# The mixers' output projection in seven products, and split input weights kept for the second half

## The chip, the core and the metric

The kernel runs on one core of one Trainium2 chip. A core has TensorE (matmuls and transposes), VectorE, ScalarE, GpSimd (POOL) and SyncE (SP, which issues most of the transfers here); each works through its own queue of instructions in order, and waits on semaphores for the others. Sixteen DMA engines move data between the device's memory (DRAM, in the program's names) and the on-chip memory. The metric is the device time of one execution in microseconds (us), median of three runs for the kernel before.

## The reference: what is computed

One decoder layer on 1024 tokens of width 1024, in float32. Four blocks follow each other, each with a residual sum and a layer norm:

```
h = LN1(a*h + 1/2 SwiGLU_1(h))                 w_gate, w_up: 1024 x 2816, w_down: 2816 x 1024
h = LN2(a*h + concat(o_a, o_b) @ w_out)        proj = h @ w_in  (1024 x 3072); w_out: 1024 x 1024
h = LN3(a*h + CrossAttention(h, LN(mem)))      4 heads of 256, 256 memory tokens; output weights w_o
h = LN4(a*h + 1/2 SwiGLU_2(h))
```

The second block is that of the "mixers". Of `proj`, 512 columns each are the query, the forget gate, the value and the output gate of a gated linear recurrence (HGRN2) with four heads of 128, and 2 x 512 are the two inputs of a spatial gate. `o_a` is the recurrence's output, normalised and multiplied by silu of the output gate; it needs every earlier token. `o_b` is the spatial gate's output, in blocks of 128 tokens. Both together, 1024 columns, go through `w_out`.

## The kernel before

Operands are held as pairs. A float32 value is split into a rounded part `hi` (type fp32r, a copy on ScalarE, line 114) and the rest `lo` (a subtraction on VectorE, line 115); a product of two such pairs is three matmuls, hi*hi, hi*lo and lo*hi, added up in PSUM (`mm3`, lines 137 to 139). The tokens' activations lie transposed in `xh[half]` and `xl[half]`, two halves of 512 tokens. Weights come through three rings of on-chip tiles: `raw` (three tiles), `whi` (six) and `wlo` (five). A tile is loaded only when the ring's oldest user is done with it.

Some large products are made with seven products of blocks in place of eight (Strassen's scheme in Winograd's form). In the two FFNs that is so for the gate, up and down projections, and in the cross attention for the output projection by `w_o` (class `Square`). For `Square` the weights' seven combined blocks are made ahead, during the first FFN, by `later`, `square_operands` and `prepare`: POOL and SP build four sums of weight blocks in DRAM (`steps`: copies on SP, accumulating transfers on POOL), and item by item a raw block is loaded (line 286), copied to `hi` and to `-hi` on ScalarE (lines 293 and 294) and written to `sq_ops` in DRAM (297); an accumulating transfer of POOL adds the raw block onto `-hi`, which gives `lo` (302). Each item, eighteen with those for the second FFN, takes 16 units of the planned time. `Square` then loads finished pairs with `fetch_parts`.

The output projection of the mixers is the plain eight. `down_group` runs over groups of token tiles, (0, 1), (2, 3, 4) and (5, 6, 7); for each of eight row blocks of `w_out` it loads and splits the block, and multiplies. So `w_out` is loaded and split three times, 24 blocks. `residual_norm` then loads the residual, adds, normalises and transposes.

The mixers go by halves, `m0` and `m1`. A "unit" is 24 matmuls of 512 columns: 24 units a half for the six groups of 512 columns. The weights of each unit or group of four are loaded and split (`load_split`) in each half, so that `w_in` is split twice. The recurrence of a head (`recurrence`) is a flow: a generator that emits its instructions a step at a time, as the units' planned time (`tick`) goes on. The order of the last part is `m1.body()`, the projection of tiles 0 and 1, `m1.tail()` (the output gate's units), `drain()` (all flows to their end), and the projection of the other tiles. Then the cross attention works on half `F = 0` first and on half `G = 1` after it.

The order of instructions on every engine is laid out when the program is built, by a planner that starts from the program's order and its own estimates of time. Instructions marked `pinned` keep their order among themselves. On the chip each queue is worked off in that order, whatever is late.

Of the kernel before, what the change touches and what calls it, by code (L numbers as in the profile page):

```python
# [15 lines left out]
P = 128  # L16
# [18 lines left out]
def hybrid_layer_kernel(ctx: ExitStack, tc: tile.TileContext, a, out):  # L35
# [184 lines left out]
    def residual_norm(tt, lag, acc, res_src, gb, bb, dst, name, keep=None):  # L220

        r = gt(f"r_{name}")
        nc.sync.dma_start(r, res_src[tt * P:(tt + 1) * P, :])
        for dh in range(2):
            sl = slice(dh * 512, (dh + 1) * 512)
            nc.vector.scalar_tensor_tensor(r[:, sl], r[:, sl], ALPHA, acc[dh], op0=ALU.mult, op1=ALU.add)
        layer_norm(r, gb, bb, name)
        nc.sync.dma_start(dst[tt * P:(tt + 1) * P, :], r)
        yield lag
        yield from to_xT_steps(r, tt, list(range(KT)), name, keep, 2.6)  # L230

    def down_group(w, nk, grp, operand, res_src, gb, bb, dst, name, keep=None):

        acc = {tt: [ps_mm(f"acc_{name}_{tt}_{dh}") for dh in range(2)] for tt in grp}
        for k in range(nk):
            wh, wl = load_split(w[k * P:(k + 1) * P, :], f"wd_{name}_{grp[0]}_{k}")
            ops = operand(grp, k)
            for tt in grp:
                oh, ol = ops[tt]
                for dh in range(2):  # L240
                    sl = slice(dh * 512, (dh + 1) * 512)
                    mm3(acc[tt][dh], oh, ol, wh[:, sl], wl[:, sl], k == 0, k == nk - 1)
            yield 1.3 * len(grp)
        for i, tt in enumerate(grp):
            spawn(residual_norm(tt, 6 + 4.5 * i, acc[tt], res_src, gb, bb, dst, f"{name}_{tt}", keep))

    def run(flow):
        for us in flow:
            tick(us)

    def xT_operand(grp, k):
        return {tt: (xh[tt // 4][:, k, (tt % 4) * P:(tt % 4 + 1) * P],
                     xl[tt // 4][:, k, (tt % 4) * P:(tt % 4 + 1) * P]) for tt in grp}

# [6 lines left out]
    def square_operands(w, ops, name):  # L261
# [11 lines left out]
        for p, first, b in ((7, 3, (0, 1)), (6, 7, (0, 0)), (4, 6, (1, 0)), (5, 1, (0, 1))):  # L273
# [4 lines left out]
                 f"{name}_{p}{n}") for p in (1, 2, 3, 7, 6, 4, 5) for n in range(2)]  # L278
# [234 lines left out]
    def strassen(wc, rhs, name):  # L513
# [26 lines left out]
        nc.vector.tensor_tensor(b0, b0, product(4), op=ALU.subtract)  # L540
        yield

    def ffn(wg, wu, wd, g, b, res_src, dst, make_xT, xf, name, start=None, h0=0):


        wc = {}
# [919 lines left out]
```

## Time and profile before

| | |
|---|---|
| runs | 2033.49, 2034.85, 2037.83 us; median 2034.85 |
| profiled execution | 2037.76 us, its span 2036.0 us |
| mean granted TensorE clock | 0.995 |
| busy share of the span | TensorE 99%, VectorE 73%, ScalarE 45%, POOL 7% |
| moved by DMA | 361.41 MB, 178 GB/s on average |
| matmuls | 9598 |

The span runs from the first to the last instruction of one execution. A matmul's busy time overlaps that of the next, so the time of many is read from a stretch, not from the sum of their durations. The wait that is put to an engine names what came last before it could go on. A waiting engine costs time only where the chain that ends last runs through it.

### The profile page before, as it was taken

How to read it: one execution, taken by the hardware profiler on the slowest of the kernel's cores; microseconds unless marked ns; L12 is line 12 of the kernel's file. 1: busy time of each engine (PE TensorE's matmuls, PEld its weight loads, DVE VectorE, ACT ScalarE, POOL GpSimd, SP SyncE). 2: the span in 40 equal slices, each digit the busy share in tenths (PEclk: the TensorE clock that was granted, in tenths of full speed). 3: DMA queues.
4: the chain of work that ended last, by engine and by line, in shares of the span. 5: the costliest groups of instructions: out<-in, count | busy, mean ns of one | idle time of the engine just before them, and what ended most of it. 6: DMA issues, size and time to landing. Idle time of an engine off the chain costs nothing.

```text
span 2036.0 us, 25494 instructions
## 1 busy us (share of the span) xinstructions
PE 2009.1 (99%) x9598; PEld 1681.2 (83%) x9598; DVE 1490.1 (73%) x2238; ACT 917.3 (45%) x1279; POOL 140.7 (7%) x187
## 2 busy tenths in 40 slices
PE   8999999999999999999999999999999999999998
PEld 7888878888887888888888888888888888888786
DVE  5977677777667967857796854678776776776688
ACT  6634344434443557647654343434333233244332
POOL 0001010120001110100110100010000000000021
PEclk9999999999999999999999999999999999999999
DMA  8369998867877642223146434652332332378874
GB/s 270 125 196 257 262 271 247 239 150 242 283 276 264 226 140 73 63 62 94 52 156 224 158 114 145 218 206 104 117 106 88 121 103 88 126 246 286 281 250 169
DMA packets 267674, 361.41 MB, mean 178 GB/s; under 512 B 16224, under 2 KB 160224, under 8 KB 267488
## 3 DMA queue, kind: packets, MB, share of 16 engines
q1 hardware_dynamic: 257216, 346.16, 50.5%
q0 software_dynamic: 10336, 13.63, 4.6%
q8 instruction: 75, 1.23, 0.2%
q14 instruction: 47, 0.39, 0.1%
HBM read 267.99 MB, written 109.58 MB: 185 GB/s over the span
## 4 chain that ended last, share of the span: by engine, by line
PE 82%; DMA 5%; DVE 4%; issue 1%; ACT 1%; POOL 0%; SPq 0%; POOLq 0%; DVEq 0%; ACTq 0%
PE dp_f L137 6%; PE dp_f L138 6%; PE dp_f L139 6%; PE st_uf L139 5%; PE st_uf L138 5%; PE st_uf L137 5%; PE st_gf L139 5%; PE st_gf L138 5%; PE st_gf L137 5%; PE psl L1168 2%; DMA wg_f_r<-in_ffn_w_gate_dram 1%; PE paq L137 1%; PE paq L139 1%; PE paq L138 1%; PE acc_mx L137 1%; PE acc_mx L138 1%
## 5 line engine op out<-in xcount | busy, mean ns | idle before, releaser
L138 PE MATMUL dp_f<-wd_f_l,ah_f 128*128 128x512 f32 x552 | 213.3, 390 | 0.0
L137 PE MATMUL dp_f<-wd_f_h,ah_f 128*128 128x512 f32 x552 | 208.5, 390 | 0.6 <-ACT ah_f L114 0.6
L139 PE MATMUL dp_f<-wd_f_h,al_f 128*128 128x512 f32 x552 | 206.1, 390 | 0.6 <-DVE al_f L115 0.5
L139 PEld LDWEIGHTS dp_f<-wd_f_h,al_f 128*128 128x128 f32 x552 | 103.6, 188 | 22.7 <-DVE al_f L115 1.4
L137 PEld LDWEIGHTS dp_f<-wd_f_h,ah_f 128*128 128x128 f32 x552 | 103.6, 188 | 22.3 <-ACT ah_f L114 1.0
L138 PEld LDWEIGHTS dp_f<-wd_f_l,ah_f 128*128 128x128 f32 x552 | 103.6, 188 | 21.4
L114 ACT ACTIVATE wd_f_h<-wd_f_r 128x1024 fp32r<-128x1024 f32 x72 | 73.2, 1022 | 99.5 <-DVE wd_f_r L651 29.1
L115 DVE TENSOR_TENSOR al_f<-ar_f,ah_f 128x1024 fp32r<-128x1024 f32 x72 | 84.5, 1174 | 27.6 <-ACT ah_f L114 27.0
L114 ACT ACTIVATE ah_f<-ar_f 128x1024 fp32r<-128x1024 f32 x72 | 73.4, 1020 | 67.0 <-DMA ar_f<-lops 64.9
L115 DVE TENSOR_TENSOR wd_f_l<-wd_f_r,wd_f_h 128x1024 fp32r<-128x1024 f32 x72 | 84.3, 1175 | 11.6 <-ACT wd_f_h L114 11.5
L137 PE MATMUL st_uf<-xh,wu_f_h 128*128 128x512 f32 x168 | 66.2, 394 | 2.7 <-ACT wu_f_h L114 2.7
L138 PE MATMUL st_uf<-xl,wu_f_h 128*128 128x512 f32 x168 | 66.0, 393 | 0.0
L139 PE MATMUL st_uf<-xh,wu_f_l 128*128 128x512 f32 x168 | 65.4, 393 | 0.1
L137 PE MATMUL st_gf<-xh,wg_f_h 128*128 128x512 f32 x168 | 65.4, 389 | 0.0
L138 PE MATMUL st_gf<-xl,wg_f_h 128*128 128x512 f32 x168 | 65.4, 389 | 0.0
L139 PE MATMUL st_gf<-xh,wg_f_l 128*128 128x512 f32 x168 | 64.7, 389 | 0.0
L775 POOL TENSOR_SCALAR nm_f<-nm_f 128x1 f32<-128x1 f32 x8 | 9.7, 1215 | 775.3 <-ACT xl L774 775.3
L531 DVE TENSOR_TENSOR top_uf<-bot_uf,st_uf 128x512 f32<-128x512 f32 x21 | 14.4, 686 | 65.5 <-PE st_uf L139 50.9
L115 DVE TENSOR_TENSOR wu_f_l<-wu_f_r,wu_f_h 128x1024 fp32r<-128x1024 f32 x42 | 51.2, 1219 | 9.7 <-ACT wu_f_h L114 9.7
L114 ACT ACTIVATE wu_f_h<-wu_f_r 128x1024 fp32r<-128x1024 f32 x42 | 44.1, 1051 | 24.2 <-issue 17.7
L529 ACT ACTIVATE bot_gf<-st_gf 128x512 f32<-128x512 f32 x21 | 12.5, 594 | 93.1 <-PE st_gf L139 93.1
L114 ACT ACTIVATE wg_f_h<-wg_f_r 128x1024 fp32r<-128x1024 f32 x42 | 44.1, 1051 | 22.2 <-PE st_gf L138 15.6
(497 smaller groups left out, 6001.0 us busy)
## 6 DMA issues: line engine op xcount, KB each, us to landing
ar_f<-lops SPq DMA_DIRECT2D x66, 512.0 KB, 5.1
wd_f_r<-in_ffn_w_down_dram SPq DMA_DIRECT2D x56, 512.0 KB, 4.9
wg_f_r<-in_ffn_w_gate_dram SPq DMA_DIRECT2D x42, 512.0 KB, 3.9
wu_f_r<-in_ffn_w_up_dram SPq DMA_DIRECT2D x42, 512.0 KB, 4.5
wd_mx_r<-in_w_out_dram SPq DMA_DIRECT2D x24, 512.0 KB, 3.9
lops<-bot_gf SPq DMA_DIRECT2D x21, 512.0 KB, 4.3
lops<-top_uf SPq DMA_DIRECT2D x21, 512.0 KB, 4.1
lops<-bot_uf SPq DMA_DIRECT2D x21, 512.0 KB, 4.7
```

Of the source, the lines that this page charges most:

```text
L114: order(nc.scalar.activation(hi, src, AF.Copy))
L115: order(nc.vector.tensor_tensor(lo, src, hi.bitcast(F32), op=ALU.subtract))
L137: nc.tensor.matmul(ps, lh, rh, start=first, stop=False, skip_group_check=more)
L138: nc.tensor.matmul(ps, lh, rl, start=False, stop=False, skip_group_check=more)
L139: nc.tensor.matmul(ps, ll, rh, start=False, stop=last, skip_group_check=more)
L529: nc.scalar.activation(b0, product(1), AF.Copy)
L531: nc.vector.tensor_tensor(t0, b0, product(2), op=ALU.add)
L775: nc.gpsimd.tensor_scalar(nmean, nmean, -1.0 / D, None, op0=ALU.mult)
L1168: nc.tensor.matmul(psl[:m, (i * NC2 + c) * 64:(i * NC2 + c + 1) * 64] .rearrange("p (n b) -> p n b", b=B), e[:, :m], blk(e, B)[:, :, 1, :] ...
```

## The change

First, the output projection becomes a `Square` named `msq`. Its left operands are the gated outputs (`o_a`, rows 0 to 511 of the contraction, and `o_b`, the rest) of the first half (kept in DRAM as `oa_dram` for use again) and of the second half. Products 2 and 1 need the first half alone and are emitted after `m1.tail()`; 7, 4, 6, 5 and 3 come after `drain()`. The second half is finished first (after product 5), the first half last (after product 3), and the cross attention takes `F = 1`, `G = 0`, so that the second half comes first there. `w_out` is no longer loaded in the mixers; its seven combined blocks, 14 items, are made in the first FFN with those of `w_o`, but with `hi` on ScalarE and `lo` on VectorE and without POOL's accumulation. With 32 items in place of 18, an item takes 12 units of planned time and the first begins 20 units earlier.

Second, the first half writes the split pairs of `w_in` to DRAM (`in_parts`), and the second half loads the pairs, with no split of its own. In the second half's body the last recurrence is started ahead of the four `vs` units, not after two of them.

```diff
-        todo = [(... ops[p - 1, n], f"{name}_{p}{n}") for p in (1, 2, 3, 7, 6, 4, 5) for n in range(2)]
+        todo = [(... ops[p - 1, n], f"{name}_{p}{n}", name == "mx") for p in (1, 2, 3, 7, 6, 4, 5) for n in range(2)]
...
         yield 16
-        for k, (src, dst, name) in enumerate(todo):
+        for k, (src, dst, name, by_vector) in enumerate(todo):
+            if by_vector:
+                hi, lo = (wpool.tile(list(src.shape), F32R, tag=f"w{i}", bufs=n, name=f"p{i}_{name}")
+                          for i, n in (("hi", 6), ("lo", 5)))
+                split(raw, hi, lo, pinned)
+                yield 3
+                for d, t in zip(dst, (hi, lo)):
+                    pinned(nc.sync.dma_start(d, t.bitcast(F32)))
+                raw = load(k + 1)
+                if steps:
+                    steps.pop(0)()
+                yield 9
+                continue
...
-            yield 4
+            yield 3
...
-            yield 12
+            yield 9
...
     def later():
-        yield 40
+        yield 20
...
-        for n, w in (("xa", a["xa_w_o"][0]),):
+        for n, w in (("mx", a["w_out"][0]), ("xa", a["xa_w_o"][0]),):
             t, s = square_operands(w, sq_ops[n], n)
-            todo += t
+            todo.append(t)
             steps += s
+        todo = todo[0][:6] + todo[1][:6] + todo[0][6:] + todo[1][6:]
...
+    def in_parts(half, view, name, key):
+        if half:
+            return fetch_parts(in_ops[key], name)
+        parts = load_split(view, name)
+        in_ops[key] = [dram.tile([P] + list(view.shape[1:]), F32, name=f"in_{name}_{i}") for i in range(2)]
+        for d, t in zip(in_ops[key], parts):
+            nc.sync.dma_start(d, t.bitcast(F32))
+        return parts
...
-            to_xT(o, self.half * NC2 + i, [0, 1, 2, 3], f"oa{self.half}{i}")
...
+            if self.half:
+                for n in range(2):
+                    if i == 0:
+                        msq.s[n] = gt(f"s3_mx{n}", (P, 2, HALF))
+                        msq.a1[0][n] = mixed_again(0, n)
+                    nc.vector.tensor_tensor(msq.s[n][:, :, cs], msq.a1[0][n][:, :, cs],
+                                            ptv[:, 2 * n:2 * n + 2, :], op=ALU.subtract)
+                    if last:
+                        msq.put(msq.s[n], 1, 0, n)
+                        msq.put(self.u[n], 1, 4, n)
+                        nc.vector.tensor_tensor(msq.s[n], msq.s[n], self.u[n], op=ALU.add)
+                return
+            split(ptv, xh[0][:, 0:4, cs], xl[0][:, 0:4, cs])
...
-    run(mix_group((0, 1)))
     play(m1.tail())
+    msq.fetch(2, 1)
+    x = msq.bank("sx2")
+    for n in range(2):
+        msq.step(2, x, 0, 4, n, True)
+    msq.p2 = msq.copies(x, "p2")
+    x = msq.bank("sx")
+    for n in range(2):
+        msq.step(1, x, 0, 0, n, True)
+    msq.fetch(7)
...
+    for t in range(4):
+        msq.residual(msq.top, 0, t)
+        msq.onto(msq.top[t][:, 0], msq.p2[t], ALU.add, ALPHA)
+        msq.onto(msq.top[t][:, 0], x[t])
+        msq.onto(msq.top[t][:, 1], x[t], ALU.subtract, ALPHA)
     drain()
-    run(mix_group((2, 3, 4)))
-    run(mix_group((5, 6, 7)))
-    F, G = 0, 1
+    for n in range(2):
+        msq.step(7, x, 1, 0, n)
+    msq.fetch(4)
+    msq.finish(x, msq.p2)
+    F, G = 1, 0
```

More of the change, by code (lines that the diff above doesn't have):

```diff
@@ L218, in layer_norm @@
         ln_apply(y, stt, gb, bb, name)
[L220 to L253, printed above, removed]
     pinned = tc.keep_in_program_order
@@ L541, in strassen, with ffn @@
         yield
-    def ffn(wg, wu, wd, g, b, res_src, dst, make_xT, xf, name, start=None, h0=0):
+    def ffn(wg, wu, wd, g, b, res_src, dst, make_xT, xf, name, start=None):
         wc = {}
@@ L1027, in feat_unit @@
     def feat_unit(half, c, name, evac):
-        evac(feat_group(load_split(wcol(w_in, c), f"{name}{half}"), half, f"ps_{name}{half}"))
+        evac(feat_group(in_parts(half, wcol(w_in, c), f"{name}{half}", c), half, f"ps_{name}{half}"))
     class Mixers:
```

53 lines of the change are left out of this document (36 added, 17 removed).

## The prediction

> **What bounds the kernel now.** I read the page first, then TensorE's waits, then the stretches of time, and last the rows of single stalls.
>
> ```profile
> span 2036.0 us, 25494 instructions
> PE 2009.1 (99%) x9598; PEld 1681.2 (83%) x9598; DVE 1490.1 (73%) x2238; ACT 917.3 (45%) x1279; POOL 140.7 (7%) x187
> q1 hardware_dynamic: 257216, 346.16, 50.5%
> q0 software_dynamic: 10336, 13.63, 4.6%
> ...
> PE dp_f L137 <- DVE db_f L798: 4.8, 2, 3.0
> PE st_uf L137 <- ACT wu_f_h L114: 2.7, 1, 2.7
> ...
> PE st_uf L137 <- DVE bot_gf L536: 0.9, 1, 0.9
> ...
> PE psl L1168 <- DVE r_mx L226: 0.4, 1, 0.4
> ```
>
> TensorE is busy 2009.1 of 2036.0 us, and of its waits one alone (0.4) lies where the mixers end. So time is saved only by giving TensorE less to do, and anything that makes it wait is paid in full. The profiled execution took 2037.76 us (1.8 around its span). It is 2.9 above the median of the three runs shown, 2034.85; I make the sum on 2037.76 and carry its difference over to the median.
>
> Now the stretches: the preparation of split operands in the first FFN, a stretch of the second FFN that has no preparation, and the mixers up to the cross attention. The columns are start and end, length, busy time of each engine, the granted clock, DMA share and GB/s.
>
> ```profile
> 102.00:177.00 75.00, 75.00 (x333) 62.10 (x332) 50.97 (x68) 29.85 (x36) 5.80 (x6) 1.00 0.77 219
> 177.00:253.00 76.00, 75.15 (x332) 61.79 (x331) 52.45 (x69) 30.26 (x37) 6.82 (x7) 1.00 0.94 257
> 253.00:303.00 50.00, 47.27 (x201) 38.28 (x200) 34.82 (x48) 24.32 (x30) 6.07 (x6) 0.97 0.96 274
> 303.00:353.00 50.00, 50.00 (x222) 41.42 (x221) 38.91 (x52) 20.16 (x25) 3.14 (x3) 1.00 0.87 237
> 353.00:454.00 101.00, 101.00 (x447) 83.62 (x446) 73.74 (x97) 47.43 (x58) 19.48 (x17) 1.00 0.78 203
> ...
> 1640.00:1740.00 100.00, 100.00 (x443) 82.81 (x442) 71.78 (x94) 32.27 (x41) 0.00 (x0) 1.00 0.30 97
> ...
> 713.00:925.00 212.00, 212.00 (x1158) 180.79 (x1158) 150.16 (x356) 125.67 (x169) 22.61 (x40) 1.00 0.27 83
> 925.00:1031.00 106.00, 106.00 (x614) 91.59 (x611) 84.30 (x218) 76.85 (x96) 9.61 (x13) 1.00 0.23 71
> 1031.00:1092.00 61.00, 60.63 (x344) 52.15 (x344) 51.74 (x114) 27.19 (x45) 7.77 (x10) 1.00 0.41 147
> ```
>
> Two things are to be seen. In the mixers the DMA engines are a quarter busy and VectorE is the fullest helper (84.3 of 106). In the first FFN, from 177 to 303, the DMA engines are full (0.94 and 0.96), and there TensorE falls to 47.27 of 50.
>
> **The products.** The output projection is 3 x 128 matmuls of 128x512 now; seven products of eight leave 336, 48 fewer. Their price is not the 390 ns that one takes from start to end, since they overlap. In a stretch with nothing else:
>
> ```profile
> L138 PE MATMUL acc_mx<-wd_mx_l,xh 128*128 128x512 f32 x128 | 50.3, 393 | 0.0
> ...
> 1104.00:1138.00 34.00, 34.00 (x151) 28.12 (x151) 3.90 (x6) 1.00 0.61 218
> L115 DVE TENSOR_TENSOR wd_mx_l<-wd_mx_r,wd_mx_h 128x1024 fp32r<-128x1024 f32 x24 | 28.9, 1218 | 7.0 <-PE acc_mx L138 4.9 <-issue 1.7 <-ACT wd_mx_h L114 0.2
> ```
>
> 34.00 us for about 150 matmuls is 0.227 each, so 48 x 0.227 = **-10.9 us**. The transposes stay as many. VectorE loses 24 splits of w_out (28.9 us) and, with the second edit, 24 splits of w_in in the second half (24 x 1.22 = 29.3), and gains 14 splits in the first FFN (17 us, where it is busy 50 to 70 of 75 to 101) and adds and subtractions of the same count as the residual work that they replace. None of this is on the path, because TensorE did not wait for it; it is cover, not gain.
>
> **The second edit's transfers.** By the page, hardware queues take 0.505 x 2036 / 346.16 = 2.97 us of all 16 engines per MB, so 1.56 for a 512 KB transfer; the accumulating queue of POOL takes 0.046 x 2036 / 13.63 = 6.9 per MB, 3.6 for 512 KB. The first half writes 48 tiles: 75 us over 212, which lifts the share from 0.27 to about 0.62. The second half reads 24 more: 37 over 167, from about 0.3 to 0.52. Each write stands on SP's queue behind VectorE's split, with the next raw loads behind it; these already wait for the same splits. I take nothing. If the cover is gone, one unit's load (4.0 us to landing, in the list of issues below) is late once: 0 to +4.
>
> **The preparation.** This is the part that I can't hide away. Before, 18 items are split in the first FFN; after, 32, begun 20 units of planned time earlier, one every 12 units in place of 16. The rows are ScalarE's first instruction of each item (durations, then the first and last start), and DMA issues with their size and their median us to landing:
>
> ```profile
> L293 ACT ACTIVATE ph_xa<-pr_xa x14: 1048/1052/1061, 122.7 to 353.0; 128x1024 fp32r<-128x1024 f32 x14
> L293 ACT ACTIVATE ph_f<-pr_f x4: 1048/1056/1065, 366.5 to 414.4; 128x1024 fp32r<-128x1024 f32 x4
> ...
> sum_xa<-in_xa_w_o_dram POOLq DMA_DIRECT2D x8, 512.0 KB, 9.7
> pr_xa<-sum_xa SPq DMA_DIRECT2D x8, 512.0 KB, 8.4
> sq_xa<-sum_xa POOLq DMA_DIRECT2D x8, 512.0 KB, 8.1
> ...
> wf_r<-in_w_in_dram SPq DMA_DIRECT2D x8, 512.0 KB, 4.0
> ```
>
> (414.4 - 122.7) / 17 = 17.2 us an item, so 12.9 after. An item of w_o is three plain transfers and one accumulating one, 3 x 1.56 + 3.6 = 8.3 us of DMA; the eight steps that form the sums are 8 x 1.56 + 8 x 3.6 = 41.3, or 5.2 an item while they last; the FFN itself takes its 0.30. All 18 items: 18 x 8.3 + 41.3 = 191 us; the stretches say 300 (shares times lengths, 102 to 454) less 0.30 x 352 = 194. The price holds.
>
> So before, the first eight items ask for 8.3 + 5.2 + 0.30 x 17.2 = 18.6 us every 17.2. At the 0.96 that was reached they run late by 2.2 each, 18 in all. After, an item of w_out is split on VectorE and has no accumulation: 4.7. The order is six of w_out, six of w_o, eight of w_out, eight of w_o, four of the FFN; the 16 steps go with the first 16. Items 1 to 6 and 13 to 16 ask for 4.7 + 5.2 + 3.9 = 13.8 every 12.9 (late by 1.4 each), items 7 to 12 for 8.3 + 5.2 + 3.9 = 17.4 (late by 5.2 each): 14 + 31 = 45 us, 27 more than before, won back only from item 17 on. What did 18 us of lateness cost TensorE?
>
> ```profile
> 199.42 0.63 SPq L286 DMA_DIRECT2D pr_xa<-in_xa_w_o_dram  x1
> 202.06 10.22 SPq L269 DMA_DIRECT2D sum_xa<-sum_xa  x2
> 212.37 0.53 SPq L123 DMA_DIRECT2D wg_f_r<-in_ffn_w_gate_dram  x1
> ...
> 281.39 1.06 ACT L293 ACTIVATE ph_xa<-pr_xa 128x1024 fp32r<-128x1024 f32 x1 [7.05 <-DMA pr_xa<-sum_xa]
> ...
> 281.48 0.39 PE L139 MATMUL st_gf<-xc4h_f,wg_f_l 128*128 128x512 f32 x1
> 284.53 0.50 PE L137 MATMUL st_uf<-xh,wu_f_h 128*128 128x512 f32 x1 [2.67 <-ACT wu_f_h L114]
> ...
> 287.03 0.63 PE L139 MATMUL st_uf<-xh,wu_f_l 128*128 128x512 f32 x1
> 287.46 0.63 PE L137 MATMUL st_uf<-xh,wu_f_h 128*128 128x512 f32 x1
> ...
> 305.66 0.39 PE L137 MATMUL st_gf<-xh,wg_f_h 128*128 128x512 f32 x1
> ```
>
> At 202.06 a copy of a sum waits on SP's queue for POOL's accumulation, about 10 us; the weight load behind it goes out at 212.37, and TensorE loses nothing. At 281.39 ScalarE's queue stands 7.05 us for a late operand; the split of the next weights is behind it, and TensorE waits 2.67. Then it runs slowly: matmuls start 0.43 apart (287.03, 287.46), and the 84 of this group last from 284.53 to 305.66, 21.1 us in place of 84 x 0.227 = 19.1. So the stall costs 2.67 + 2.1 = 4.8, and with the 0.9 at another place the lateness cost 5.7 of its 18 us. On the clock the Trainium skill (TensorE: Matmul & The Clock Gate, What's actually happening) says that an idle window of about 3.4 us halves the clock until a busy window has passed. By that rule a 2.67 us gap need not slow anything, and the stall would be 2.67; the row shows it slowed, with the granted clock at 0.97 over these 50 us, so the row decides.
>
> After, nothing to 27 us more could reach TensorE; below nothing too, to -5.7, if lighter items end even the old stall. POOL's lateness mostly falls on sums that are loaded 60 us or more later, and the 10 us at 202.06 were absorbed. But the copies of w_o's sums now wait for POOL behind six accumulating items, so about twice as long. I take **one more stall of the kind seen, +4.8**.
>
> **Where the mixers end.** The seven products need the second half's gated outputs sooner and normalise the second half's tokens just ahead of the attention's queries.
>
> ```profile
> L1236 PE MATMUL po<-vt,bs x64: 270/275/328, 803.1 to 1082.4; 128*128 128x128 f32 x64
> L1245 DVE SCALAR_TENSOR_TENSOR ot<-po,hrs,ngb x32: 340/343/351, 808.5 to 1086.2; 128x128 f32<-128x128 f32 x32
> ...
> 1358.19 0.39 PE L139 MATMUL sy_xa<-s_xa_h,xl 128*128 128x512 f32 x1
> ...
> 1365.64 1.27 DVE L386 SCALAR_TENSOR_TENSOR r_xa<-r_xa,rs_xa,b_xa 128x1024 f32<-128x1024 f32 x1
> ...
> 1384.29 0.48 PE L137 MATMUL pg_f<-xh,wg_f_h 128*128 128x512 f32 x1
> ```
>
> The last recurrence's outputs leave VectorE 4 us after its last matmul (1082.4 to 1086.2). Gating, transposes, eight subtractions and one split follow, some 10 us, estimated from the 1218 ns of 1024 columns on VectorE. Over it lie two products from the first half, 96 x 0.227 = 21.8 us, and the last recurrence starts two units earlier. I take 0; uncovered it would be up to 14.
>
> The cross attention's own square shows the other handover. Product 5 ends at 1358.4, the last norm of its tokens at 1366.9: 8.5 us, and 2.3 for transposes and a split make 10.8. The cover after is product 3 alone, 48 x 0.227 = 10.9, and the transposes. I take 0, at most +12: in that row the consumer started 25.9 us after product 5, 12 more than 10.9 and 2.8 of transposes, but behind a second product.
>
> **Sum:** -10.9 + 4.8 + 0 + 0 = -6.1: 2031.7 on the profiled execution's scale, **2028.8** on the median's.
>
> **The rivals.** *The preparation stays hidden* (0.23): the copies' waits are absorbed like the one at 202.06: -10.9, 2024. For it: 10 us without loss. Against it: the stall at 281.39 with less to do. *The DMA engines become the bound in the first FFN* (0.25; the other side): 27 us more of lateness, in-order on SP and ScalarE, starve the weight splits between 170 and 300. It decides once more than 10.9 / 27 = 0.40 of it reaches TensorE; before, 5.7 / 18 = 0.32 did. At 0.6 it is +16, so net +5, 2040; in full +27, 2051. For it: shares of 0.94 and 0.96 already. Against it: lateness that sits in POOL's sums hurts nobody. *The handover to the queries stalls* (0.14): half its bound, +6, on top of the forecast: no change, 2035. For it: VectorE has every norm of the second half there; against it: the chain of 10.8 just fits. The Trainium skill (DMA: Bandwidth & Descriptors, Queues, rings and completion order) has each DMA engine serve its queues in turn, packet by packet. That speaks for the second rival, since weight loads then take turns with accumulations; no run here separates that from mere fullness.
>
> **How the numbers follow.** Forecast 0.38, with its own range 2026 to 2032. 0.2% is 4.1 us, about what a measurement of this kernel tells from no change. Faster by more: 0.32 of the forecast's 0.38, and the hidden case's 0.23: 0.55. Within: 0.06 from the forecast, 0.10 from the handover, 0.08 from full DMA engines: 0.24. Slower: 0.17 and 0.04, 0.21. For 8 in 10 the range goes from 2021 (the hidden case with part of the old 5.7 won back) to 2041 (0.6 of the lateness).
>
> **What would show it.** TensorE's matmuls fall by 48. The stretch from the mixers' start to the queries is shorter by about 11. In the first FFN the DMA share stays over 0.9 from about 150 on, and TensorE's waits there grow from 3.6 to 6 or 7 us, behind an operand of the preparation. A wait before the first query or the seventh product of over 3 us, or waits over 10 in the first FFN, prove the forecast wrong.

## The result, and the profile after

The changed kernel takes **2110.28 us** (2107.05 to 2110.87) against 2034.85: a ratio of 1.0377, with a 95% interval of 1.0357 to 1.0396. It is 75 us slower, where 6 us less was forecast and 2041 was the top of the range. The profiled execution has a span of 2109.2 us and a mean granted clock of 0.98.

The page of the kernel after, the lines that answer those shown of before (busy time, and the two kinds of DMA queue with packets, MB and share):

```profile
span 2109.2 us, 25638 instructions
PE 2021.2 (96%) x9550; PEld 1681.5 (80%) x9550; DVE 1469.2 (70%) x2226; ACT 901.8 (43%) x1277; POOL 154.7 (7%) x199
q1 hardware_dynamic: 266080, 416.42, 56.7%
q0 software_dynamic: 12512, 17.83, 5.9%
```

TensorE has its 48 matmuls less (9550 for 9598), and it is now idle for 88 us of the span, 27 before. Its waits in the kernel after (what waited, for what; total, times, longest):

```profile
PE st_gf L137 <- ACT wg_f_h L114: 21.3, 2, 16.4
PE dp_f L137 <- ACT ah_f L114: 12.4, 6, 4.5
PE st_uf L139 <- DVE wu_f_l L115: 10.7, 2, 10.0
PE pt_mx L164 <- DVE xl L115: 7.6, 3, 4.7
PE pt_mx L164 <- DVE mv_mx L202: 3.7, 1, 3.7
PE sx_mx L137 <- DVE r_mx L345: 3.4, 1, 3.4
```

Three places are to be seen: the gate and up projections of the first FFN (`st_gf`, `st_uf`), its down projection (`dp_f`), and the mixers' end (`sx_mx`, and `pt_mx`, the transposes for the queries). The starts of the first matmuls of each stage, by the names of their tiles, put the loss there as well (us):

| stage | before | after |
|---|---|---|
| start to the down projection (first `dp_f`) | 496.1 | 536.4 |
| down projection, to the mixers (first `ps_wiv`) | 217.1 | 238.7 |
| mixers without their output projection, to the last `ps_wg` | 356.8 | 352.9 |
| output projection and handover, to the first query (`paq`) | 91.5 | 106.8 |
| cross attention, to the second FFN (first `pg_f`) | 222.8 | 226.6 |
| second FFN | 651.7 | 647.8 |

(In before, the 21.8 us from 1030.9 that 96 products took ahead of the last `ps_wg` are counted with the projection.) So +40 and +22 in the first FFN. In the projection it is +15 where 10.9 less work is done, a loss of 26. The mixers' 4 less and the cross attention's 4 more cancel. The second FFN, in which nothing was changed, is 4 shorter.

The stretches of the kernel after that answer those of before, with three new ones (columns as in the prediction):

```profile
102.00:177.00 75.00, 74.70 (x328) 61.20 (x327) 60.71 (x78) 31.14 (x39) 4.72 (x5) 1.00 0.93 288
177.00:253.00 76.00, 70.26 (x302) 57.15 (x302) 50.38 (x68) 32.56 (x39) 6.96 (x7) 0.98 0.97 282
253.00:303.00 50.00, 33.65 (x139) 27.20 (x138) 20.01 (x25) 13.41 (x17) 5.76 (x6) 0.83 0.77 186
303.00:353.00 50.00, 39.89 (x168) 32.16 (x167) 30.27 (x40) 15.04 (x19) 3.57 (x4) 0.90 0.98 283
353.00:454.00 101.00, 101.00 (x448) 83.62 (x446) 72.79 (x97) 45.40 (x55) 4.21 (x4) 1.00 0.81 245
500.00:600.00 100.00, 88.43 (x365) 70.50 (x365) 60.54 (x70) 41.83 (x44) 14.61 (x13) 0.95 1.00 317
1150.00:1175.00 25.00, 20.24 (x84) 15.98 (x83) 21.87 (x29) 5.18 (x5) 0.00 (x0) 0.93 0.77 308
1200.00:1250.00 50.00, 37.99 (x166) 30.48 (x165) 41.93 (x53) 21.17 (x34) 14.46 (x20) 0.80 0.37 126
```

The worst stretch, 253 to 303, isn't the one with the fullest DMA engines: TensorE is busy 33.65 of 50 us there at a DMA share of 0.77, and loses nothing from 353 on at 0.81. It waits for something that is in line behind something else. The chain can be followed in time, queue by queue. POOL after, its accumulating transfers (in brackets the idle time before; "issue" means that the profile shows nothing it waited for):

```profile
238.96 1.06 POOL L279 DMA_DIRECT2D sq_xa<-in_xa_w_o_dram  x1 [8.68 <-issue]
247.57 1.06 POOL L279 DMA_DIRECT2D sq_xa<-in_xa_w_o_dram  x1 [7.55 <-DMA wg_f_r<-in_ffn_w_gate_dram]
257.13 0.90 POOL L234 DMA_DIRECT2D sum_xa<-in_xa_w_o_dram  x1 [8.49 <-issue]
263.55 0.91 POOL L234 DMA_DIRECT2D sum_xa<-in_xa_w_o_dram  x1 [5.51 <-issue]
```

SP after, the issues of the same time (start, and the time from there to the end of the row's last issue):

```profile
263.25 8.03 SPq L234 DMA_DIRECT2D sum_xa<-sum_xa  x2
271.38 0.53 SPq L123 DMA_DIRECT2D wg_f_r<-in_ffn_w_gate_dram  x1
...
276.34 0.48 SPq L251 DMA_DIRECT2D pr_mx<-sum_mx  x1
```

ScalarE after, and then TensorE after:

```profile
285.28 1.06 ACT L114 ACTIVATE phi_mx<-pr_mx 128x1024 fp32r<-128x1024 f32 x1 [21.82 <-DMA pr_mx<-sum_mx]
```

```profile
287.34 0.80 PE L137 MATMUL st_gf<-xh,wg_f_h 128*128 128x512 f32 x1 [16.35 <-ACT wg_f_h L114]
287.93 0.63 PE L138 MATMUL st_gf<-xl,wg_f_h 128*128 128x512 f32 x1
...
291.77 0.57 PE L139 MATMUL st_gf<-xh,wg_f_l 128*128 128x512 f32 x1
292.18 0.39 PE L137 MATMUL st_gf<-xh,wg_f_h 128*128 128x512 f32 x1
...
319.33 0.79 PE L139 MATMUL st_uf<-xh,wu_f_l 128*128 128x512 f32 x1 [9.96 <-DVE wu_f_l L115]
```

A copy of a sum of `w_o` on SP needs the accumulation before it, which POOL works off one by one behind those of the items. What SP waited for at the head of its queue from 240 to 276 in the kernel after, and from 195 to 224 in the kernel before, around the copy at 202.06 (total, times, longest):

```profile
SPq L234 <- DMA sum_xa<-in_xa_w_o_dram: 24.5, 2, 17.5
```

```profile
SPq L269 <- DMA sum_xa<-in_xa_w_o_dram: 11.1, 2, 9.2
```

So SP stood 24.5 us in place of 11.1, most of it ahead of the row at 263.25. Two things behind the copies came late. The next block of gate weights is issued at 271.38 and lands 8.7 us later, at 280.1. The load of the next item, 276.34, lands for 285.28, and until then ScalarE's queue stands 21.82 us at the item's first copy, with the split of those weights behind it. TensorE waits 16.35, from 271.0 on. As an estimate from these times, about 10 of the 16 are the late weights, which could not be used before 281.3 in any order, and about 6 are ScalarE's order. The next copy that needs POOL (299.8; SP stood 17.6 us for its two halves) ends in the 9.96, this time over VectorE: it stands 15.66 us for the weight block that is issued at 308.16 and lands at 317.4, with the subtraction that TensorE needs behind it.

### The profile page after: what moved, and what is told of

Its sections match the earlier page's. It is cut to its first block, busy times and chain, and to the rows that moved or that the text cites. A ratio compares the mean times of both kernels' runs of the same rounds, so it can differ in the third digit from the quotient of the medians.

```text
span 2109.2 us, 25638 instructions
## 1 busy us (share of the span) xinstructions
PE 2021.2 (96%) x9550; PEld 1681.5 (80%) x9550; DVE 1469.2 (70%) x2226; ACT 901.8 (43%) x1277; POOL 154.7 (7%) x199
## 4 chain that ended last, share of the span: by engine, by line
PE 76%; DMA 9%; DVE 6%; issue 5%; ACT 2%; SPq 1%; POOL 1%; POOLq 0%; DVEq 0%; ACTq 0%
PE st_gf L139 5%; PE st_gf L138 5%; PE st_gf L137 5%; PE st_uf L138 5%; PE st_uf L137 5%; PE st_uf L139 5%; PE dp_f L137 4%; PE dp_f L138 4%; PE dp_f L139 4%; PE psl L1181 2%; PE paq L137 1%; PE paq L138 1%; PE paq L139 1%; DMA wd_f_r<-in_ffn_w_down_dram 1%; DMA wd_f_t<-rops 1%
## 5 line engine op out<-in xcount | busy, mean ns | idle before, releaser
L137 PE MATMUL dp_f<-wd_f_h,ah_f 128*128 128x512 f32 x552 | 214.3, 397 | 15.0 <-ACT ah_f L114 12.4
L139 PE MATMUL dp_f<-wd_f_h,al_f 128*128 128x512 f32 x552 | 197.3, 390 | 1.3 <-DVE al_f L115 1.2
L139 PEld LDWEIGHTS dp_f<-wd_f_h,al_f 128*128 128x128 f32 x552 | 103.6, 188 | 24.5 <-DVE al_f L115 3.0
L115 DVE TENSOR_TENSOR al_f<-ar_f,ah_f 128x1024 fp32r<-128x1024 f32 x72 | 84.4, 1174 | 32.2 <-ACT ah_f L114 31.7
L115 DVE TENSOR_TENSOR wd_f_l<-wd_f_r,wd_f_h 128x1024 fp32r<-128x1024 f32 x72 | 84.2, 1175 | 16.9 <-ACT wd_f_h L114 16.7
L137 PE MATMUL st_gf<-xh,wg_f_h 128*128 128x512 f32 x168 | 67.5, 402 | 21.4 <-ACT wg_f_h L114 21.3
L139 PE MATMUL st_uf<-xh,wu_f_l 128*128 128x512 f32 x168 | 66.0, 396 | 10.8 <-DVE wu_f_l L115 10.7
L115 DVE TENSOR_TENSOR wg_f_l<-wg_f_r,wg_f_h 128x1024 fp32r<-128x1024 f32 x42 | 51.2, 1219 | 14.4 <-ACT wg_f_h L114 14.4
L137 PEld LDWEIGHTS st_gf<-xh,wg_f_h 128*128 128x128 f32 x168 | 32.6, 194 | 29.3 <-ACT wg_f_h L114 22.6
L115 DVE TENSOR_TENSOR wu_f_l<-wu_f_r,wu_f_h 128x1024 fp32r<-128x1024 f32 x42 | 51.2, 1218 | 5.9 <-ACT wu_f_h L114 5.9
```

Of the source, the lines that this page charges most:

```text
L115: order(nc.vector.tensor_tensor(lo, src, hi.bitcast(F32), op=ALU.subtract))
L137: nc.tensor.matmul(ps, lh, rh, start=first, stop=False, skip_group_check=more)
L139: nc.tensor.matmul(ps, ll, rh, start=False, stop=last, skip_group_check=more)
```

## The experiments

Differences are against the kernel before on the same chip.

**One edit alone.** The kernel before with the kept split weights only:

```diff
...
-        evac(feat_group(load_split(wcol(w_in, c), f"{name}{half}"), half, f"ps_{name}{half}"))
+        evac(feat_group(in_parts(half, wcol(w_in, c), f"{name}{half}", c), half, f"ps_{name}{half}"))
```

> The kernel before with the second edit alone: the first half writes the split w_in, the second half loads the pairs; the projection stays in eight products. Theory A (all of the loss comes from w_out's preparation and from the new end of the mixers): within 4 us of before. Rival (the 25 MB of writes and 12.6 MB more of reads cost too): 5 to 20 us slower, with TensorE waits between 713 and 1092.

Measured: 2035.35 against 2034.92, ratio 1.0002 [0.9988, 1.0016]. The second edit costs nothing and brings nothing that could be told from no change (-2.4 to +3.3 us by the interval).

**The changed kernel without the items of `w_out`,** at the pace of before:

```diff
-        for n, w in (("mx", a["w_out"][0]), ("xa", a["xa_w_o"][0]),):
+        for n, w in (("xa", a["xa_w_o"][0]),):
...
-        yield 20
+        yield 40
...
-    msq = Square(sq_ops["mx"], res[0], (None, None), res[1], "mx", 0,
+    msq = Square(sq_ops["xa"], res[0], (None, None), res[1], "mx", 0,
```

> The changed kernel with the 14 items of w_out left out of the first FFN, with the pace of before (16 units an item, begun after 40); the seven products take w_o's blocks in their place, so the preparation of w_out is what is left out. Theory A (w_out's items cost the 62 us by which the first FFN is longer): mixers begin at 713 to 716 in place of 775, total 2048. Rival (the FFN's loss has another cause, such as the planner's order): they begin after 740, total over 2070. The loss of some 22 us where the mixers end stays in both.

Measured: 2048.25, +13.3, ratio 1.0071 [1.0047, 1.0096]. The mixers begin at 716.3, 713.2 before. So the fourteen items and the new pace cost 75.4 - 13.3 = **62 us**, nearly all of the loss in the first FFN. The handovers' loss is left: 107 us from the last `ps_wg` to the first query, as in the kernel after.

**The sums of `w_o` six items later,** so that their copies on SP don't come while POOL is behind:

```diff
+        steps[6:6] = [lambda: None] * 6
```

> The changed kernel, but no sum step goes with items 7 to 12 (w_o's accumulating items); the last ten steps come six items later. Work and bytes are the same. Theory B (the sum copies that wait on SP's queue for POOL are what starves TensorE): the waits of 16.4, 10.0 and 5.0 us in the first FFN fall to below 5 in sum, 25 to 35 us faster than the changed kernel, 2075 to 2085. Rival C (the DMA engines are simply asked for too much): the lateness is only moved, less than 10 us gained.

Measured: 2082.77, ratio 1.0233 [1.0203, 1.0262], 27.5 us less than the changed kernel. The down projection begins at 508.3 in place of 536.4, so all of it comes from the gate and up projections (28 in the profiled execution). TensorE's waits in this run:

```profile
PE dp_f L137 <- ACT ah_f L114: 12.8, 8, 4.2
...
PE st_gf L137 <- ACT wg_f_h L114: 5.7, 4, 3.5
```

The waits of 16.4 and 10.0 are gone, and SP has no wait for a sum left; the wait of the down projection isn't gone. The two stretches in which the kernel after lost most, in this run:

```profile
253.00:303.00 50.00, 49.85 (x220) 40.97 (x219) 36.47 (x48) 20.92 (x27) 2.87 (x3) 1.00 0.99 298
303.00:353.00 50.00, 49.50 (x216) 40.00 (x216) 38.80 (x49) 18.65 (x24) 3.80 (x5) 1.00 1.00 295
```

The bytes are the same, and the DMA engines are fuller here than in the kernel after (0.77 and 0.98), yet TensorE loses 0.15 and 0.5 us of 50. So in these stretches it was the order of the queues, and not full DMA engines.

**All items split by VectorE,** none by POOL's accumulation; POOL keeps the sums:

```diff
-                 f"{name}_{p}{n}", name == "mx") for p in (1, 2, 3, 7, 6, 4, 5) for n in range(2)]
+                 f"{name}_{p}{n}", True) for p in (1, 2, 3, 7, 6, 4, 5) for n in range(2)]
```

> The changed kernel with all 32 items split by ScalarE and VectorE, so that POOL accumulates sums alone: 18 accumulating transfers of 512 KB, about 65 us of all DMA engines by the page's rates, are gone, and VectorE has 18 splits more. Theory B (POOL's queue is the cause): its queue is never more than one step late, the waits in the first FFN fall to under 8 us, total 2050 to 2060. Rival C (demand as such): items ask for about 1.07 of the time in place of up to 1.34, so about two thirds of the 62 us come back, total near 2070. If VectorE becomes the bound instead: no gain, with waits on VectorE.

Measured: 2063.32, ratio 1.0142 [1.0113, 1.0171], 47 us less than the changed kernel. Down projection from 498.1, mixers from 727.7. The first and the last of POOL's sixteen accumulations for the second FFN's items, in the kernel after, and the last one in the kernel before:

```profile
516.80 1.18 POOL L279 DMA_DIRECT2D f_ops<-in_ffn_w_gate_dram  x1 [16.01 <-DMA f_ops<-pn_f]
...
618.09 1.15 POOL L279 DMA_DIRECT2D f_ops<-in_ffn_w_up_dram  x1 [4.85 <-issue]
```

```profile
448.74 1.15 POOL L302 DMA_DIRECT2D f_ops<-in_ffn_w_up_dram  x1 [2.86 <-issue]
```

In the kernel after they run 82 us into the down projection (from 536.4), and the DMA share is 1.00 from 500 to 600. Each of the sixteen moves 128 KB, a quarter of what one for `w_o` moves, and yet lands in 3.9 to 9.2 us, 6.2 on the median, against 8.5 for 512 KB. Without these accumulations the last write of the preparation is issued at 518.7, and the wait of `dp_f` for `ah_f` is 7.0. The down projection takes 229.6 us, 238.7 in the kernel after and 217.1 before, so the accumulations are about 9 of the 22 lost there. How they reach it isn't shown: the blocks `ar_f` that it loads land in 6.8 us on the median between 500 and 620 in the kernel after, 5.2 before, as full DMA engines would have it.

**The handovers, and the pace,** each alone on top of the last kernel: the transposes of the first half later; the operands of the sums and the residuals loaded ahead of the last units; the steps spread over the items, which come every 11 units in place of 12.

```diff
-                spawn(self.norm(self.top[t], f, t, 8 + 2.5 * t))
+                spawn(self.norm(self.top[t], f, t, (8 if p2 is None else 24) + 2.5 * t))
```

> The kernel with all items split by VectorE, and the first half's norms of the projection leave 24 units of planned time, not 8, before their transposes. Theory D (TensorE's queue holds a transpose of a first-half tile ahead of the first query and waits for that tile's norm): the wait of 3.7 us for that norm goes, and part of the 7.7 for VectorE's splits with it; from the last output-gate unit to the first query 108 us becomes 100 to 103, total 2056 to 2059. Rival (VectorE is full there and the second half's own norms are late): 0 to 2 us gained.

```diff
-                        msq.a1[0][n] = mixed_again(0, n)
...
+    msq.a1[0].update({n: mixed_again(0, n) for n in range(2)})
+    for t in range(4):
+        msq.residual(msq.top, 0, t)
     play(m1.tail())
...
-        msq.residual(msq.top, 0, t)
```

> The kernel with all items split by VectorE, and the stored outputs and residual tiles of the projection are loaded ahead of the output-gate units, not after the weights of product 7 on SP's queue. Theory E (product 7 waits because VectorE gets these tiles late, behind weight loads that wait for slots): the waits of product 7's stretch (3.4, 1.3 and 0.8 us, and the slow clock after) go, 5 to 8 us gained, total 2055 to 2058. Rival (the chain of gating, subtractions and splits is what is late): less than 2 gained.

```diff
-                yield 9
+                yield 8
...
+        for i in (4, 7, 10, 13, 16, 19):
+            steps.insert(i, lambda: None)
```

> The kernel with all items split by VectorE; the 16 sum steps are spread over the first 22 items, and an item takes 11 units of planned time in place of 12, so that the last is done before the down projection begins. Theory (its remaining loss in the FFN, 14 us, is the tail of the items beside the down projection's first loads): mixers begin at 716 to 720 in place of 728, total 2052 to 2056. Rival (the faster pace only fills the DMA engines earlier): gate and up stage longer by 3 to 8 us, total 2060 or more.

Measured: 2057.55, ratio 1.0116 [1.009, 1.0141]; 2052.41, 1.0093 [1.007, 1.0116]; 2055.0, 1.01 [1.0072, 1.0129]; the kernel before here 2032.46. The intervals lie close to that of the kernel without them, so the stages tell more: from the first product to the first query it is 106.3 us without, 98.4 with later transposes (the wait on `mv_mx`, 3.7, is gone) and 96.3 with early loads (that on `r_mx`, 3.4, is gone). With the spread steps the mixers begin at 723.1 in place of 727.7, later than the 716 to 720 expected; the down projection takes 223.5 in place of 229.6.

**All of these together:**

> The three edits on the kernel with all items split by VectorE together: spread steps and 11 units, operands ahead, first-half norms later. If each theory holds they add up: 2063 less 4 to 7, 5 to 8 and 7 to 11, 2037 to 2047, level with the kernel before or just above. Below 2035 only if the handovers cost less than 10 us together, since the sum of the seven products saves 10.9.

Measured: 2042.8 (2036.39 to 2048.2), ratio 1.0045 [1.0029, 1.0061]; 89.8 us to the first query. Still slower than before, with 6.1 of wait at the queries. VectorE in this run, as that wait begins:

```profile
1153.26 1.23 DVE L115 TENSOR_TENSOR xl<-pt_mx,xh 128x512 fp32r<-128x512 f32 x2
1154.41 1.27 DVE L208 SCALAR_TENSOR_TENSOR r_mx<-r_mx,mv_mx,g_mx 128x1024 f32<-128x1024 f32 x1
1155.61 1.27 DVE L198 BATCH_NORM_STATS2 st_mx<-r_mx 128x6 f32<-128x512 f32 x2
1156.80 0.67 DVE L115 TENSOR_TENSOR xl<-pt_mx,xh 128x512 fp32r<-128x512 f32 x1
```

The splits that the queries need (L115) have the norms of the first half (L198, L208) between them, which nobody needs yet. Hence two more runs. **The first half's statistics kept behind the second half's last splits:**

```diff
-                split(ptv, *dst)
+                split(ptv, *dst, pinned if name.startswith('mx') and half else lambda ins: ins)
...
+                if self.later:
+                    yield 12 + 2.5 * t
-                layer_norm(y, self.gb, self.bb, n)
+                layer_norm(y, self.gb, self.bb, n, pinned if self.later else lambda ins: ins)
...
-                spawn(self.norm(self.top[t], f, t, (8 if p2 is None else 24) + 2.5 * t))
+                spawn(self.norm(self.top[t], f, t, 8 + 2.5 * t if p2 is None else 14))
```

> The kernel of e8_together (2042.8) with the first half's statistics kept behind the second half's last splits on VectorE's queue. Theory (VectorE's queue order is what remains of the loss at the queries): in e8_together three norms of the first half, about 4 x 1.27 us each with their two passes of statistics, stand among the last six splits that the queries need, and the last of these splits starts some 8 us late; without them the last split leaves 5 to 8 us sooner, TensorE's wait of 6.1 us behind it shrinks to under 2, the stretch from the first product to the first query goes from 89.8 to 81 to 84, and the time to 2034 to 2038. Rival (the chain add, norm, transpose, split of the second half's last tile is itself longer than product 3): the wait stays over 4 us and the time between 2040 and 2044.

**And the same without the items of `w_out`:**

> The kernel of e2_no_w_out_items (2048.25) with the three edits of the handovers: operands and residuals loaded ahead, first half's norms later, their statistics behind the second half's splits. It leaves out the preparation of w_out's blocks in the first FFN, like e2_no_w_out_items. Theory (seven products are worth their 10.9 us, and preparation and handovers ate it): the handovers give back 98.4 or 106 to about 82 from the first product to the first query, some 20 us, and the time is 2026 to 2030, 4 to 8 below the kernel before. Rival (part of the loss is in the projection itself: more VectorE work and slower matmuls beside it): it stays at or above the kernel before, 2034 to 2040.

Measured: 2039.08, ratio 1.0031 [1.0016, 1.0047], and 2028.92, ratio 0.9978 [0.9969, 0.9988]. The wait at the queries is the same row in both:

```profile
PE pt_mx L164 <- DVE xl L115: 4.4, 3, 3.3
```

The norms in between were only a small part: 88.4 us to the first query in both, not 81 to 84, and the wait stays over 4. The rival of that run is nearer, that the second half's own chain of add, norm, transpose and split outlasts product 3; no run shortens that chain, so it isn't shown. The second run, which leaves out the preparation of `w_out`, shows what the products are worth when nothing has to be prepared for them: 4.4 us less than before, at the low end of the 4 to 8 expected.

**The preparation moved into the mixers,** first without and then with the kept split weights:

```diff
...
+    spawn(prepare(*square_operands(a["w_out"][0], sq_ops["mx"], "mx")))
     play(m0.head())
```

> The kernel of e10_no_items_mended with the preparation of w_out back, but in the mixers in place of the first FFN (fourteen items on VectorE, 15 units of planned time each, sums by POOL as before), and without the split input weights kept for the second half. The whole computation is there. Theory (the first FFN's full DMA engines made the preparation dear; where they are a quarter busy it is hidden): the first FFN stays as before, the mixers' stretch from first matmul to last stays within 4 us of its 352, and the time is 2027 to 2033, below the kernel before. Rival (rings of split tiles and VectorE, 84 of 106 us busy in the second half, are as short in the mixers): the mixers' stretch grows by 8 to 25 us, and the time is 2037 to 2055.

> The kernel of e11_items_in_mixers with the split input weights kept for the second half, as in the change. By the prices of the prediction the first half's writes ask for 0.35 of the DMA engines on top of 0.27, the items for 9.9 us every 21, 0.47: some 1.1, so over what there is in the first half. Theory (full DMA engines are what makes the preparation dear): slower than e11_items_in_mixers by 3 to 15 us, with waits in the mixers' first half. Rival (only POOL's sums ahead of other transfers, not the share, make TensorE wait; or VectorE is what is short, and the kept splits relieve it): within 2 us of it, or faster.

Measured: 2078.67, ratio 1.0219 [1.0197, 1.0242], and 2092.75, ratio 1.029 [1.0269, 1.031]. The first theory fell: the mixers take 401.6 us, far over the rival's 8 to 25 as well. Two stretches of the first of these runs:

```profile
765.00:815.00 50.00, 45.13 (x213) 37.42 (x214) 32.38 (x71) 32.68 (x36) 4.20 (x6) 0.90 0.74 193
815.00:865.00 50.00, 45.28 (x236) 38.01 (x236) 34.45 (x76) 28.88 (x38) 1.76 (x3) 0.90 0.47 159
```

TensorE loses as much at a share of 0.47 as at 0.74. What SP waited for at the head of its queue in the mixers of this run, the largest row:

```profile
SPq L263 <- ACT phi_mx L114: 176.6, 14, 23.4
```

The write of an item stands 12.6 us on average for ScalarE's copy, with loads of weights behind it. With the kept weights it is another 14 us, within the 3 to 15 expected for full DMA engines (0.99 from 765 to 815); that SP has more to do there is not told apart from it.

**Is it SP's queue?** Three runs to take SP's waits away: the writes later in the mixers, the writes later in the first FFN, and the preparation's transfers issued by POOL.

```diff
-                yield 3
+                yield 8
...
-                yield 12
+                yield 7
```

> The kernel of e11_items_in_mixers (2078.7) with the writes of each item 8 units of planned time behind its split in place of 3 (and 7 in place of 12 to the next). In e11_items_in_mixers the mixers last 401.6 us in place of 352 with the DMA engines only half busy, and SP's queue stands 176.6 us in front of these writes, waiting for ScalarE's copy. Theory (a write that waits at the head of SP's queue keeps back the weights behind it, which makes ScalarE's next copy later still): with the writes later these waits fall under 70 us, the mixers last 355 to 378, the time is 2033 to 2056. Rival (VectorE, ScalarE and the rings of tiles are short in the mixers, and SP's waits only show it): the mixers stay over 390 us and the time over 2066.

```diff
-                yield 3
+                yield 6
...
-                yield 8
+                yield 5
```

> The kernel of e9_norms_later (2039.1) with the writes of each item in the first FFN 6 units behind its split in place of 3 (and 5 in place of 8 to the next). Theory (SP's wait at these writes, some 130 us there, is what is left of the preparation's 10 us): half of it comes back, 2032 to 2036. Rival (there the ring of split tiles, held longer by each item, or the full DMA engines are what is left): no gain or a loss, 2038 to 2046.

```diff
-                pinned((nc.gpsimd if op else nc.sync).dma_start(dst[rows], src[rows], **op))
+                pinned(nc.gpsimd.dma_start(dst[rows], src[rows], **op))
...
-            pinned(nc.sync.dma_start(raw, src))
+            pinned((nc.sync if name[:2] == "f2" else nc.gpsimd).dma_start(raw, src))
...
-                    pinned(nc.sync.dma_start(d, t.bitcast(F32)))
+                    pinned(nc.gpsimd.dma_start(d, t.bitcast(F32)))
```

> The kernel of e9_norms_later (2039.1) with the preparation's loads, writes and copies of sums issued by POOL in place of SP (the loads of the four items of the second FFN stay on SP). The bytes are the same. Theory (in-order waiting on SP's queue is what the preparation costs): the first FFN runs as in e10_no_items_mended, the mixers begin at 708 to 714, the time is 2029 to 2034. Rival (the DMA engines' fullness is the cause, whoever issues): the mixers begin at 718 to 726 as before, 2037 to 2043; or POOL, which issues one transfer after another, falls behind, the preparation reaches far into the down projection, and the time is over 2045.

Measured: 2078.38, ratio 1.0229 [1.0202, 1.0256]; 2035.89, ratio 1.0015 [1.0002, 1.0029]; 2076.68, ratio 1.0211 [1.0193, 1.023]. The first is inconclusive: SP's waits at the writes were 152.7 us in place of 176.6, so the edit hardly took them away, and the mixers took 399 us. The second is 3 us below its base, with an interval that overlaps, and SP's waits there did not shrink either (80.8 for 78.0 at the copies for `w_out`): nothing follows. The third did take the preparation off SP, and lost 37 us against its base, nearly all in the gate and up projections (down projection from 538.0, base 503.0). The time is that of the last rival, over 2045, but not for its reason: the last write of the preparation is issued at 514.6, ahead of the down projection. ScalarE's waits there, in the run with POOL issuing:

```profile
ACT phi_mx L114 <- DMA pr_mx<-sum_mx: 35.1, 6, 11.7
...
ACT phi_xa L114 <- DMA pr_xa<-sum_xa: 20.1, 4, 12.7
ACT phi_xa L114 <- DMA pr_xa<-in_xa_w_o_dram: 17.9, 3, 10.0
ACT phi_mx L114 <- DMA pr_mx<-in_w_out_dram: 17.2, 3, 9.9
```

POOL in this run, around one pair of accumulations (`sum_mx`), and a stretch of it:

```profile
155.25 0.95 POOL L234 DMA_DIRECT2D sum_mx<-in_w_out_dram  x1 [0.68 <-issue]
164.65 0.91 POOL L234 DMA_DIRECT2D sum_mx<-in_w_out_dram  x1 [8.45 <-issue]
165.25 0.90 POOL L263 DMA_DIRECT2D sq_mx<-phi_mx  x1
165.82 0.87 POOL L263 DMA_DIRECT2D sq_mx<-plo_mx  x1
173.33 0.74 POOL L251 DMA_DIRECT2D pr_mx<-in_w_out_dram  x1 [6.64 <-issue]
```

```profile
150.00:200.00 50.00, 41.51 (x159) 33.55 (x160) 33.63 (x42) 17.55 (x21) 10.51 (x17) 0.86 0.78 245
```

The loads of the next item now stand behind POOL's accumulations and come late, and ScalarE stands for them 90 us in all, with the weights' splits behind it. TensorE falls to 41.51 of 50 at a DMA share of 0.78. So SP's queue isn't the cause by itself, nor are full DMA engines: it is an operand that comes late by whatever queue, and an engine's order behind it. In the base, ScalarE's waits for items have about half that sum and none over 7.7 us, and in the kernel after one had 21.82.

## Why the prediction was wrong, step by step

**The products** hold as far as they can be seen: 48 matmuls fewer. Net of what the handovers cost even when mended, 4.4 of the 10.9 was measured.

**The second edit's transfers** were right: 0 taken, 0.4 measured, with nothing to tell it from 0.

**The preparation** is the step that failed: "one more stall of the kind seen, +4.8" was 62. The queue was the right one: "the copies of w_o's sums now wait for POOL behind six accumulating items". Even "about twice as long" was right, 24.5 us of SP's time for 11.1. What failed is the price. I sized the lateness by the DMA engines' capacity (27 us more in all) and turned it into stalls by the share that had reached TensorE before, 5.7 of 18. Both are means, and what counts is the longest single one. Before, SP stood 11.1 us for POOL and nothing was lost, and ScalarE stood 7.05, of which 2.67 reached TensorE. After, ScalarE stood 21.82 and 16.35 reached TensorE. So 4.4 and 5.5 us were covered, and the rest came through whole. The three longest waits of the gate and up projections, 16.35, 9.96 and 4.95 (21.3 less 16.35), with 1.4 to 2.4 us of slow matmuls behind each, make 37 of the 40 us lost there. Moving the sums away gave 27.5 of it back.

The other part was not in the sum at all. My own 12.9 us an item put the last of 32 items 31 x 12.9 = 400 us behind the first, so at about 502, past the 496.1 at which the down projection began; the stretches that I sized ended at 454. And I took accumulations as DMA work, 3.6 us of all engines for 512 KB, and not as a queue. An item of the second FFN moves its 512 KB in four accumulations; the last four items' sixteen follow each other every 6.75 us on POOL, from 516.80 to 618.09, so such an item holds POOL's queue for 27 us. So the end of the preparation stands beside the down projection: +22, of which 9 went with the accumulations and 6 more with an earlier end of the items (229.6 to 223.5).

**Where the mixers end** failed too: 0 taken, 26 lost. "None of this is on the path" was read off TensorE's waits in the kernel before, in which eight products lie there; I took no count of VectorE's work between product 5 and the queries. Sums, two halves of norms, splits for transposes and five splits of the queries' weights lie there together; from 1200 to 1250 VectorE is busy 41.93 of 50 while TensorE has 37.99, at a granted clock of 0.80. The bound of +12 for the queries was too low: early loads ahead of product 7 gave back 10.0 of the 26 (106.3 to 96.3), which leaves about 16 for the queries. The 0 came from one chain of 10.8 against a cover of 10.9 and the +12 from one row of the cross attention's own square, not from everything in VectorE's line here. The gating's handover (up to 14 if uncovered) came out nearly free, with a wait of 0.8, but product 7 waited for operands that SP loads only behind weights that wait for ring tiles: not a case I had named (early loads took that wait of 3.4 away).

**The rivals.** The one on the other side came true in direction and beyond its price: 2051 in full, 2110 measured. Its mechanism, DMA engines as the bound, is not what held the gate and up projections back: with the sums later TensorE loses 0.15 of 50 us at a share of 0.99, and with the items in the mixers, or issued by POOL, 4.7 to 8.5 of 50 at shares of 0.47 to 0.78. In the down projection, at 1.00, it stays possible. "The handover to the queries stalls" came on top, not instead. The hidden case fell. Of the signs named, the 48 matmuls came; the stretch from the mixers' start to the queries is 11 us longer (459.7 for 448.3), not 11 shorter; and a wait over 10 in the first FFN, named as the proof against the forecast, came with 16.35.

The sum in the runs' terms: 62.1 for the items (changed kernel less the one without them), 17.7 for what the three edits at the handovers give back (13.3 and -4.4), and -4.4 for the products, which by difference still lose 6.5 of their 10.9. That is 75.4.

No kernel here with the whole computation beats the one before; the best, 2035.89, ratio 1.0015 [1.0002, 1.0029], is at most 0.3% slower. What stays open: how the accumulations reach the down projection; which of SP's and ScalarE's order holds the mixers back when they carry the items, since the runs meant to part them left the waits in place; and whether accumulations that are spaced still further would make the preparation free.

## What to carry to other kernels

Work that is added "beside" a full engine goes through in-order queues, and costs by its longest single lateness, not by its mean: follow each added instruction to what it waits for and what stands behind it, on every queue, to the end of the backlog and not only to the end of the stage. A transfer type that its queue works off one at a time is priced by its spacing on that queue, so by how many transfers there are, and not by its bytes or its share of the DMA engines. And before a stage loses work on the bounding engine, count the helper's whole list in the window that shrinks.

## What the runs showed of the hardware that was not expected

Accumulating transfers from DRAM to DRAM never overlapped on POOL. In the kernels before and after, 84 of them in all, the next one starts 0.26 us or more after the one before has landed, and in 58 of the 82 gaps 0.35 us or less after it. The one at 263.55, for instance, lands 7.2 us later, at 270.8, and the next starts at 271.10. Landing took 6.1 to 12.1 us for 512 KB and still 3.7 to 9.2 for 128 KB. Plain transfers on the same queue are not held at once: in the run with POOL issuing, two start 0.60 and 0.57 behind an accumulation (164.65, 165.25, 165.82), and the third only at 173.33, 0.3 after that accumulation has landed. Whether the chip or the program's own waits hold the queue the traces don't say; they put most of it down to "issue".

The slow clock after a stall did not grow with the stall. After 2.67 us of waiting, the kernel before lost 2.1 beside it; after 16.35 us, the rows at 287.34 to 292.18 show 11 matmuls in 4.84 us in place of 11 x 0.227 = 2.5, so 2.3; after 9.96 it was 1.8 and after 4.95 1.4. A wait of 3.03 us in the kernel before, at 618.93, was followed by no slow matmul at all. The Trainium skill (TensorE: Matmul & The Clock Gate, What's actually happening) has the full clock come back after a busy window of about 3.4 us, wherever it falls; 4.84 us fits one such window with a late start. The 2.67 us wait slowed the clock where that page asks for about 3.4 us idle, and the 3.03 us wait agrees with it. The mean granted clock of 0.83 over the 50 us from 253 holds mostly the wait: the matmuls ran slow for 4.84 us of it, and half speed for that long alone would make 0.95 (an estimate).
